# A hybrid decoder block on one core: the last two products of the first up-projection columns trade places, and the weight parts of the first three projections begin at one place

## The chip, the cores and the metric

The kernel runs on one core of a Trainium2 chip. The metric is device time in microseconds (us): the median of several runs of the whole kernel.

## What is computed

One layer of a decoder trunk over 256 tokens and 16 meta tokens (272 rows), width 2048, all in float32. Cut to what matters here:

```python
u = rms_norm(h, g_pre_mix)                      # 272 x 2048
proj = u @ w_in                                 # 2048 x 7168
z_pool, v_conv, g_conv, gate_a, gate_b = split(proj)   # 1024, 1024, 1024, 2048, 2048 columns
y_a = causal_multiscale_pool(z_pool) @ w_pool_out
y_b = conformer_conv(v_conv, g_conv) @ w_conv_out      # 31 taps, layer norm, swish
m = sigmoid(gate_a) * y_a + sigmoid(gate_b) * y_b
h = h + rms_norm(m @ w_o)
f = square(relu(rms_norm(h) @ w_up)) @ w_down   # 2048 x 8192, 8192 x 2048
h = h + rms_norm(f)
```

## The kernel before, in words

**Split numbers.** A float32 matrix is used as two parts. `hi` is the value rounded to a shorter format by a copy on ScalarE (line 178); `lo` is the rest, by a subtraction on VectorE (line 181). A product of two split matrices is the sum of three matmuls: hi times hi, hi times the rest of the activation, lo times hi.

**The stream of weights.** All weights come in the order of one list, `stream` (lines 111 to 134), in chunks of 1 MB (128 partitions by 2048 numbers). `open_chunk` (line 159) takes the next chunk, loads it on SyncE's queue into one of three `raw` buffers, and notes the two split steps; `fetch` (line 198) opens chunks two ahead of the one that it hands out and issues their split steps. The parts live in six rooms, three for `hi` and three for `lo`, used in turn (keys `hi0`, `hi1`, `hi2`, `lo0`, ...). So a chunk's `hi` can be written as soon as TensorE has finished with the chunk three before it.

**Places.** A room is 48 numbers longer than a part, so that the part can begin at one of four offsets. `LINE` is 16 numbers, 64 bytes. `part_tile` (line 152) shifts the part inside the room so that its start, counted in lines of 64 bytes and modulo four (256 bytes), has a chosen value, the same in every room; call it the part's place. Line 155 reads the pair (place of `hi`, place of `lo`) from the table `PLACES`; a chunk that is not in the table gets (1, 1). Line 141 gives every chunk of `w_up` the pair (2, 1). Line 142 gives the first 24 chunks pairs of their own: two chunks make one product of 256 columns, and the product with number p gets (p mod 4, p // 4). The rows of the activation `u` are padded so that all of them begin at one place too.

**The first three projections** are those products: 256 columns each of `v` (convolution values), `g` (convolution gate) and `z` (pool). Their order and their places are

| product | v0 | g0 | v1 | g1 | v2 | g2 | v3 | g3 | z0 | z1 | z2 | z3 |
|---|---|---|---|---|---|---|---|---|---|---|---|---|
| (hi, lo) | 0,0 | 1,0 | 2,0 | 3,0 | 0,1 | 1,1 | 2,1 | 3,1 | 0,2 | 1,2 | 2,2 | 3,2 |

Here the weights stand in the array and the 272 rows of `u` stream past. Each product is 16 blocks of depth by 2 column tiles by 3 matmuls (`mm3`, line 334: `hi` with u's first part, `hi` with its second, `lo` with its first), so 96 matmuls with 272 moving columns. v0 runs interleaved with the transposes that make `u` (lines 442 to 452); the others run in `project` (line 362). Beside them, VectorE works through a list of pending pieces, `drain` handing out one piece after another at points of the program that are fixed when it is built: 240 taps of the convolution (line 405) and the sums of the pooling windows, among others.

**What follows** is a run of wide products (gates, pool and convolution outputs, `w_o`), where the activation stands and 512 weight columns stream (`block_t`, line 590), all with parts at (1, 1); then the MLP, in four passes of `w_up` and `w_down`.

**The up projection** has the weights standing again. The two parts of an activation lie side by side, so that one wide matmul (`mm2_high`, line 342: 512 moving columns) gives both products with `hi`, and a narrow one (`mm2_low`, line 348: 256 columns) adds the product with `lo` to the first half of the accumulator. `mm2` (line 353) issues the wide one and then the narrow one. The first 512 columns of the first pass, `up00`, are written out by hand (lines 892 to 945), because their activation becomes ready piece by piece; their last quarter of the depth is the loop of lines 940 to 945. There each of four accumulators gets four pairs, wide and narrow, and is then evacuated: `halves` (line 378) copies the first half on ScalarE and adds the second on VectorE.

Of the kernel before, what the change touches and what calls it, by code (L numbers as in the profile page):

```python
# [14 lines left out]
P = 128  # L15
# [7 lines left out]
def hybrid_block(ctx: ExitStack, tc: tile.TileContext, ins: dict, out: bass.AP):  # L23
# [7 lines left out]
    KD = D // P  # L31
# [28 lines left out]
    def acc_tile(name):  # L60
        return psA.tile([P, CW], F32, tag="acc", name=name)
# [15 lines left out]
    def flush(n=0):  # L77
        while len(late) > n:
            late.pop(0)()
# [20 lines left out]
    def columns(w, k0, nk, c0, shape=(CK, CW)):  # L100

        ck, cw = shape
        return [(w[(k0 + kc) * P:(k0 + kc + ck) * P, c0:c0 + cw]
                 .rearrange("(k p) c -> p k c", p=P), shape) for kc in range(0, nk, ck)]
# [6 lines left out]
    stream = []  # L111
# [2 lines left out]
            stream += columns(w_in, 0, KD, c0 + h * HALF_CW, HALF)  # L114
    for h in range(PW // HALF_CW):
        stream += columns(w_in, 0, KD, h * HALF_CW, HALF)
    first_products = len(stream)
    standing_chunks = set()
    for n in range(2 * D // CW):
        stream += columns(w_in, 0, KD, G0 + n * CW)  # L120
# [14 lines left out]
    FIRST = KD // HALF[0]  # L135
# [3 lines left out]

    LINE = 16  # L140
    PLACES = {n: (2, 1) for n in standing_chunks}
    PLACES.update({n: (n // FIRST % 4, n // FIRST // 4) for n in range(first_products)})
    KEYS = [f"{tag}{b}" for tag in ("lo", "hi") for b in range(3)]
    ready = {}

# [52 lines left out]
    def fetch(ahead=2):  # L198

        for c in range(ahead + 1):  # L200
            if c == len(opened) and at["n"] < len(stream):
                open_chunk()
            if c < len(opened):
                split_pieces(c)
        flush()
        return opened.pop(0)[:2]
# [135 lines left out]
    def mm2_high(acc, hi, act, k, cs, start, ts=slice(0, T), stop=False):  # L342
        off = act.shape[3] - T
        nc.tensor.matmul(acc.rearrange("p (a t) -> p a t", a=2)[:, :, ts], hi[:, k[0], cs],  # L344
                         act[:, k[1], :, off + ts.start:off + ts.stop], start=start, stop=stop,
                         skip_group_check=True)

    def mm2_low(acc, lo, act, k, cs, stop=False):
        off = act.shape[3] - T
        nc.tensor.matmul(acc[:, :T], lo[:, k[0], cs], act[:, k[1], 0, off:],  # L350
                         start=False, stop=stop, skip_group_check=True)

    def mm2(acc, hi, lo, act, k, cs, first, last):


        mm2_high(acc, hi, act, k, cs, first, stop=last)
        mm2_low(acc, lo, act, k, cs, stop=last)
# [291 lines left out]
    hi, lo = fetch()  # L649
    for g in range(NG):  # L650
        for j in range(GK):
            q = g * GK + j
            acc = acc_tile(f"acc_grp_{q}")[:, :T]
# [158 lines left out]
    u2 = m  # L812
# [28 lines left out]
    def evac_up(j0):  # L841
        def f(j, acc):
            s = halves(acc, f"up_{j0 + j}")
            nc.vector.scalar_tensor_tensor(s, s, 0.0, s, op0=ALU.max, op1=ALU.mult)
            split(f_act[(j0 + j) // (KD // 2)], (j0 + j) % (KD // 2), s)
        return f
# [89 lines left out]
    hi, lo = fetch()  # L936
# [3 lines left out]
    for j, acc in enumerate(accs):  # L940
        for k in range(CK):
            kk = 3 * CK + k
            mm2(acc, hi, lo, u2, (k, kk), slice(j * P, (j + 1) * P), False, kk == KD - 1)
        flush(1)
        evac_up(0)(j, acc)
    ssq2 = const.tile([P, NT, NB], F32, name="ssq2")
# [64 lines left out]
    n = KD // CK - 3  # L1011
    for kc in range(n):
        hi, lo = fetch()
# [54 lines left out]
```

## Time and profile before

| | |
|---|---|
| median of 3 runs | 1237.76 us (1237.73 to 1237.81) |
| the profiled execution: its own time | 1238.2 us |
| its span, first to last instruction | 1236.3 us |
| TensorE matmuls (PE): busy | 1224.7 us (99%), 6572 instructions |
| VectorE (DVE): busy | 807.6 us (65%) |
| ScalarE (ACT): busy | 541.9 us (44%) |
| mean granted clock of TensorE | 0.998 |

The profile lists instructions with start and duration. A matmul's duration is longer than its step: the next one starts before it ends. What a row of matmuls costs is therefore read from start to start, or from the chain of work that ended last, which follows each instruction back to what released it and gives every stretch its length. A busy share says little here: the question is how fast TensorE steps, and whether anything makes it wait.

### The profile page before, as it was taken

How to read it: one execution, taken by the hardware profiler on the slowest of the kernel's cores; microseconds unless marked ns; L12 is line 12 of the kernel's file. 1: busy time of each engine (PE TensorE's matmuls, PEld its weight loads, DVE VectorE, ACT ScalarE, POOL GpSimd, SP SyncE). 2: the span in 40 equal slices, each digit the busy share in tenths (PEclk: the TensorE clock that was granted, in tenths of full speed). 3: DMA queues.
4: the chain of work that ended last, by engine and by line, in shares of the span. 5: the costliest groups of instructions: out<-in, count | busy, mean ns of one | idle time of the engine just before them, and what ended most of it. 6: DMA issues, size and time to landing. Idle time of an engine off the chain costs nothing.

```text
span 1236.3 us, 15686 instructions
## 1 busy us (share of the span) xinstructions
PE 1224.7 (99%) x6572; PEld 1061.3 (86%) x6572; DVE 807.6 (65%) x938; ACT 541.9 (44%) x571; POOL 6.2 (0%) x18
## 2 busy tenths in 40 slices
PE   9999999999999999999999999999999999999997
PEld 7999988888888888898888888888888888888886
DVE  5799988999676654585654556654475544556555
ACT  6533334444584433555433345433344433435432
POOL 1000000000000000000000000000000000000000
PEclk9999999999999999999999999999999999999999
DMA  8655556556548656646556566556566556566551
GB/s 260 207 181 179 171 171 204 188 188 204 175 165 298 212 205 204 204 142 200 175 200 197 183 199 200 180 199 200 185 194 204 182 193 204 176 201 203 187 187 68
DMA packets 130757, 237.22 MB, mean 192 GB/s; under 512 B 3985, under 2 KB 29905, under 8 KB 130160
## 3 DMA queue, kind: packets, MB, share of 16 engines
q1 hardware_dynamic: 128768, 229.78, 57.4%
q0 software_dynamic: 768, 4.35, 0.9%
q10 hardware_dynamic: 1152, 2.11, 0.5%
q8 instruction: 51, 0.84, 0.3%
q14 instruction: 18, 0.15, 0.0%
HBM read 234.12 MB, written 2.10 MB: 191 GB/s over the span
## 4 chain that ended last, share of the span: by engine, by line
PE 98%; DVE 1%; DMA 0%; ACT 0%; DVEq 0%; issue 0%; ACTq 0%
PE acc_dn L595 26%; PE acc_up L344 19%; PE acc_gate L595 14%; PE acc_up L350 10%; PE acc_o L595 5%; PE acc_v L339 4%; PE acc_z L339 4%; PE acc_g L339 4%; PE acc_co L595 4%; PE acc_po L595 4%; PE acc_f_last L595 2%; PE acc_o_last L595 2%; DMA x_in<-in_x_dram 0%; PE xt L286 0%; PE ht L820 0%; PE mt L715 0%
## 5 line engine op out<-in xcount | busy, mean ns | idle before, releaser
L181 DVE TENSOR_TENSOR lo<-raw,hi 128x2048 fp32r<-128x2048 f32 (+1 forms) x236 | 495.1, 2101 | 354.5 <-ACT hi L178 354.1
L178 ACT CAST hi<-raw 128x2048 fp32r<-128x2048 f32 (+1 forms) x236 | 413.7, 1757 | 559.3 <-PE acc_dn L595 190.6
L344 PE MATMUL acc_up<-m,hi 128*128 128x512 f32 (+1 forms) x1008 | 339.1, 387 | 0.0
L595 PE MATMUL acc_dn<-hi,f_act 128*128 128x512 f32 x960 | 296.3, 389 | 0.0
L350 PE MATMUL acc_up<-m,lo 128*128 128x256 f32 x992 | 272.5, 277 | 0.0
L344 PEld LDWEIGHTS acc_up<-m,hi 128*128 128x128 f32 x1008 | 187.0, 188 | 39.5
L595 PEld LDWEIGHTS acc_dn<-hi,f_act 128*128 128x128 f32 x960 | 180.2, 188 | 37.5
L595 PE MATMUL acc_dn<-lo,f_act 128*128 128x512 f32 x480 | 186.8, 389 | 0.0
L350 PEld LDWEIGHTS acc_up<-m,lo 128*128 128x128 f32 x992 | 185.2, 188 | 0.1
L595 PE MATMUL acc_gate<-hi,u 128*128 128x512 f32 x512 | 158.6, 390 | 0.0
L405 DVE SCALAR_TENSOR_TENSOR c<-a,taps,c 128x256 f32<-128x256 f32 x240 | 115.4, 483 | 6.6
L595 PEld LDWEIGHTS acc_gate<-hi,u 128*128 128x128 f32 x512 | 96.1, 188 | 20.0
L595 PEld LDWEIGHTS acc_dn<-lo,f_act 128*128 128x128 f32 x480 | 90.1, 188 | 18.5
L595 PE MATMUL acc_gate<-lo,u 128*128 128x512 f32 x256 | 99.6, 389 | 0.0
L595 PE MATMUL acc_o<-hi,m 128*128 128x512 f32 x192 | 59.6, 390 | 0.0
L595 PEld LDWEIGHTS acc_gate<-lo,u 128*128 128x128 f32 x256 | 48.1, 188 | 10.0
L339 PE MATMUL acc_v<-u,hi 128*128 128x272 f32 x256 | 50.6, 295 | 0.0
L339 PE MATMUL acc_z<-u,hi 128*128 128x272 f32 x256 | 48.6, 289 | 0.0
L339 PE MATMUL acc_g<-u,hi 128*128 128x272 f32 x256 | 48.1, 288 | 0.0
L595 PEld LDWEIGHTS acc_o<-hi,m 128*128 128x128 f32 x192 | 36.0, 188 | 7.4
L595 PE MATMUL acc_co<-hi,s_act 128*128 128x512 f32 x128 | 40.4, 391 | 0.0
L339 PEld LDWEIGHTS acc_z<-u,hi 128*128 128x128 f32 x256 | 40.4, 188 | 0.0
(222 smaller groups left out, 1060.8 us busy)
## 6 DMA issues: line engine op xcount, KB each, us to landing
raw<-in_w_up_dram SPq DMA_DIRECT2D x64, 1024.0 KB, 5.4
raw<-in_w_down_dram SPq DMA_DIRECT2D x64, 1024.0 KB, 5.1
raw<-in_w_in_dram SPq DMA_DIRECT2D x54, 1024.0 KB, 5.1
raw<-in_w_o_dram SPq DMA_DIRECT2D x16, 1024.0 KB, 5.1
raw<-in_w_pool_out_dram SPq DMA_DIRECT2D x8, 1024.0 KB, 5.1
raw<-in_w_conv_out_dram SPq DMA_DIRECT2D x8, 1024.0 KB, 5.2
raw<-in_w_in_dram SPq DMA_DIRECT2D x8, 256.0 KB, 7.7
h<-in_x_dram POOLq DMA_DIRECT2D x1, 2048.0 KB, 11.0
```

The source lines that it names most:

```text
L178: nc.scalar.copy(hi[:, sl, :], raw[:, sl, :])
L181: nc.vector.tensor_sub(lo[:, sl, :], raw[:, sl, :], f32(hi[:, sl, :]))
L339: nc.tensor.matmul(acc, w[:, k[0], cs], act[:, k[1], a, off:], start=first and n == 0, stop=last and n == 2)
L344: nc.tensor.matmul(acc.rearrange("p (a t) -> p a t", a=2)[:, :, ts], hi[:, k[0], cs], act[:, k[1], :, off + ts.start:off + ts.stop], start ...
L350: nc.tensor.matmul(acc[:, :T], lo[:, k[0], cs], act[:, k[1], 0, off:], start=False, stop=stop, skip_group_check=True)
L405: nc.vector.scalar_tensor_tensor(c, conv["a"][:, q, i:i + T], taps[:, q, i:i + 1], c, op0=ALU.mult, op1=ALU.add)
L595: nc.tensor.matmul(acc, act(kk)[:, a_, ts_], w_[:, k, :], start=kk == 0 and n == 0, stop=kk == nk - 1 and n == 2)
```

## The change

The table's second line goes, so that the first 24 chunks get (1, 1) like the rest of the stream. And in the last quarter of `up00`, the last of the four pairs of each accumulator is issued narrow first, then wide; the wide matmul now closes the accumulation.

```diff
     for h in range(PW // HALF_CW):
         stream += columns(w_in, 0, KD, h * HALF_CW, HALF)
-    first_products = len(stream)
     standing_chunks = set()
...
     PLACES = {n: (2, 1) for n in standing_chunks}
-    PLACES.update({n: (n // FIRST % 4, n // FIRST // 4) for n in range(first_products)})
     KEYS = [f"{tag}{b}" for tag in ("lo", "hi") for b in range(3)]
...
     for j, acc in enumerate(accs):
         for k in range(CK):
             kk = 3 * CK + k
-            mm2(acc, hi, lo, u2, (k, kk), slice(j * P, (j + 1) * P), False, kk == KD - 1)
+            cs = slice(j * P, (j + 1) * P)
+            if kk < KD - 1:
+                mm2(acc, hi, lo, u2, (k, kk), cs, False, False)
+            else:
+                mm2_low(acc, lo, u2, (k, kk), cs)
+                mm2_high(acc, hi, u2, (k, kk), cs, False, stop=True)
         flush(1)
         evac_up(0)(j, acc)
```

No instruction is added or taken away. On TensorE four pairs change their order; on the other engines and the queues the order of instructions is what it was. In the changed order the narrow matmul of the first such pair waits for ScalarE's part of the activation and the wide one for VectorE's, where before the wide one waited for both.

## The prediction

> **What bounds the kernel now.** I read the page's chain of work that ended last first, then the same chain in order of time over the first 165 us, where the first three projections run, then what the engines waited for.
>
> ```profile
> PE 98%; DVE 1%; DMA 0%; ACT 0%; DVEq 0%; issue 0%; ACTq 0%
> ```
>
> TensorE's own sequence makes up 98% of the span. A change pays if TensorE steps faster or waits less, and almost nothing else counts. The list of what TensorE waited for shows how little waiting there is to remove:
>
> ```profile
> PE idle L272 <- POOL ident masks.py:199: 1.4, 1, 1.4
> PE xt L286 <- DMA x_in<-in_x_dram: 1.1, 1, 1.1
> PE acc_grp L339 <- DVE y L658: 0.4, 1, 0.4
> ```
>
> Two waits come before the first product and one at 343 us; none is touched by the change. So the question is the step from one matmul to the next. The chain in order of time (start, length, what, count):
>
> ```profile
> 25.51 3.20 PE acc_v L339 x24
> 28.71 12.04 PE acc_g L339 x96
> 40.75 6.05 PE acc_v L339 x48
> 46.80 0.96 PE pb L329 x6
> 47.76 3.03 PE acc_v L339 x24
> 50.80 0.19 PE pv_pool_scale L243
> 50.98 0.61 PE taps_t L464 x8
> 51.59 3.22 PE acc_v L339 x24
> 54.81 12.05 PE acc_g L339 x96
> 66.86 12.14 PE acc_v L339 x96
> 79.01 11.85 PE acc_g L339 x96
> 90.85 12.09 PE acc_v L339 x96
> 102.94 12.05 PE acc_g L339 x96
> 114.99 48.58 PE acc_z L339 x384
> ```
>
> Each x96 row is one product: 96 matmuls of one shape, with 272 moving columns. They are not equally long. g2 takes 11.85 us, 123.4 ns a step; the others 12.04 to 12.15 (z: 48.58 / 4), 125.4 to 126.5 ns. g2 is the product with places (1, 1). So the kernel before holds a table of twelve pairs of places with their times, and the changed kernel uses for all twelve the pair with the shortest row.
>
> **The change, part one: the places.** What is removed is the difference of each product to g2; nothing is added. From the rows, less 11.85: g0 0.19, g1 0.20, v2 0.29, v3 0.24, g3 0.20, g2 nothing, and the four z products 48.58 - 47.40 = 1.18. v1 is cut in three by other work; at 123.4 ns its 48 matmuls would take 5.92 in place of 6.05 (0.13), its 24 take 2.96 in place of 3.03 (0.07); the last 24 follow transposes and carry a restart that stays, so I give them the 0.07 of the equal piece before: 0.27 in all. Together 2.57 us.
>
> v0 is interleaved with transposes. Its plain step stands at its end, after the last transpose; the first and the last row of this stretch of the timeline (start, duration, engine, line), with the first of g0:
>
> ```profile
> 25.91 0.41 PE L339 MATMUL acc_v<-u,hi 128*128 128x272 f32 x2
> ...
> 28.42 0.29 PE L339 MATMUL acc_v<-u,lo 128*128 128x272 f32 x1
> 28.54 0.41 PE L339 MATMUL acc_g<-u,hi 128*128 128x272 f32 x2
> ```
>
> From 25.91 to 28.54 lie 21 matmuls, 125.2 ns each. At 123.4 the 96 of v0 would save 0.17 us if all were plain. Some follow a transpose and are not; the bounds are 0 and 0.17, and I take 0.13, since most steps are plain. Part one: 2.70 us.
>
> Does the gain reach the end? What could hold TensorE up in its place is VectorE, which works beside it on the convolution. From 54.65 to 163.41 us (length, busy), and what it waited for there:
>
> ```profile
> 54.65:163.41 108.76, 101.69 (x156) 1.00 0.53 171
> ```
>
> ```profile
> DVE lo L181 <- ACT hi L178: 3.5, 6, 0.7
> DVE v L412 <- PE acc_v L339: 1.1, 1, 1.1
> DVE g L419 <- PE acc_g L339: 0.3, 1, 0.3
> ```
>
> In this stretch TensorE would gain 0.20 + 0.29 + 0.24 + 0.20 + 1.18 = 2.11 us, and VectorE has 4.9 us of waits for others to give up. It stays just ahead. Nor is a short lateness felt, because the parts are early. The `lo` of one chunk, and the start of z2, which reads it:
>
> ```profile
> 127.06 1.91 ACT L178 CAST hi<-raw 128x2048 fp32r<-128x2048 f32 x1 [4.14 <-PE acc_z L339]
> ```
>
> ```profile
> 129.06 2.28 DVE L181 TENSOR_TENSOR lo<-raw,hi 128x2048 fp32r<-128x2048 f32 x1
> ```
>
> ```profile
> 139.09 0.41 PE L339 MATMUL acc_z<-u,hi 128*128 128x272 f32 x2
> ```
>
> It is done at 131.34 and first read from 139.09 on: 7.7 us of cover. ScalarE stood idle for 4.14 us until TensorE gave the room free, so the load had landed; the loads are no bound either. If VectorE's cover were gone, each later `lo` would cost TensorE its lateness, which is the third rival below. Behind z the chain is TensorE's again: what comes later starts 2.7 us earlier and is as long as before.
>
> Here the Trainium skill speaks against the change. "TensorE: Matmul & The Clock Gate", section "Step-by-step: what each phase is for", says that TensorE reads moving data and weights through two independent ports, so that loading the next weights takes no bandwidth from the running matmul. By that rule the place of the weights should be without effect and the sum would be that of part two alone, near 1237.7 us. The trace disagrees as far as it goes, with 123.4 against 125.4 to 126.5 ns for equal matmuls; no run here shows the ports themselves.
>
> **Part two: the swap.** Four times, "wide, narrow" becomes "narrow, wide". The order before this pair is ...narrow, and behind it comes the next accumulator's wide one. So a step wide to narrow goes, a step narrow to narrow comes, and a step wide to wide comes in place of one narrow to wide.
>
> ```profile
> 533.10 1.92 PE acc_up L350 x16
> ...
> 544.02 0.23 PE acc_up L344
> 544.25 0.12 PE acc_up L350
> 544.38 0.23 PE acc_up L344
> 544.61 0.12 PE acc_up L350
> ```
>
> ```profile
> 617.51 87.06 PE acc_dn L595 x384
> ```
>
> In the mixed order a wide step is 0.23 and a narrow one 0.12 us (x16 narrow: 1.92, the same 0.12). A row of wide ones, with other operands, has 87.06 / 384 = 0.227. So the pair costs the same by the first rows, and some 0.006 us less by the last; four times is 0 to -0.03. In a wide to wide step at this stage the next weights could be read less well, but the trace has no such step; bounded by the nearest difference, that of the places (some 3 ns), it is +0.01. I take -0.02, which does not move the first decimal.
>
> The new waits cost nothing: the pieces of u2 in question are written by VectorE here, before the loop begins at 543.86.
>
> ```profile
> 541.66 1.66 DVE L830 SCALAR_TENSOR_TENSOR m<-ht,vecs,m 128x256 fp32r<-128x256 f32 x4
> ...
> 543.86 0.39 PE L344 MATMUL acc_up<-m,hi 128*128 128x512 f32 x1
> 544.09 0.28 PE L350 MATMUL acc_up<-m,lo 128*128 128x256 f32 x1
> ```
>
> They end at 543.32. The evacuation now waits for a wide matmul that starts 0.12 after its narrow one and lasts 0.39 (0.51), where it waited for a narrow one that starts 0.23 after and lasts 0.28 (0.51): no difference.
>
> **The sum.** -2.70 - 0.02 = -2.7 us. The profiled execution took 1238.2 us by its own time (span 1236.3), 0.4 above the median of the runs; with the change it would be 1235.5 (span 1233.6). Against the median, 1237.76 - 2.7 = 1235.1 us.
>
> **The rivals.**
>
> 1. *The place is not the cause.* Only one product stands at (1, 1), and it might owe its time to when it runs. Then only part two counts: 1237.7. Against it: g0, g1 and g3 run with less and more beside them and agree within 0.01 us, so what lies beside hardly matters, while g2 between them differs by 0.2. Chance 5%. (The skill's rule of two ports, above, comes out here.)
>
> 2. *One pair, but not in every room.* g2 used two of the three rooms; how the third does at (1, 1) with this shape is not shown. If it steps like the average of the rest, 8 of 24 chunks gain nothing: 1237.76 - 1.8 = 1236.0. Against it: the wide products use all three rooms at (1, 1) in rotation, and 384 of them average 0.227 without a hitch. 6%.
>
> 3. *VectorE becomes the bound.* If some of its waits are hand-over times that it can't give up, it falls behind by up to 2.1 us, and if the cover did not absorb that, half of the gain would go: 1236.4. Against it: 7.7 us of cover, and VectorE waits again for 7.7 us in all between 163 and 203 us, where it would catch up:
>
> ```profile
> DVE lo L181 <- ACT hi L178: 7.7, 6, 3.1
> ```
>
> 8%.
>
> 4. *Slower: writes meet reads.* While g2 ran, the `hi` being written stood at place 2. In the changed kernel ScalarE and VectorE write parts at the very places from which TensorE reads. If such a meeting cost as much as the worst place costs over the best (126.5 - 123.4 = 3.1 ns) on top of the worst, a step would be 129.6 ns: (129.6 - 126.0) x 1152 matmuls = 4.1 us more, 1241.9. It turns slower than before once the mean step passes 126 ns. Against it: the wide products write and read at (1, 1) already. In the gate stage, with VectorE busy for nearly all of the time, and in the down projection, with far less beside it, they step alike: 146.91 / 648 and 87.06 / 384 are both 0.2267.
>
> ```profile
> 163.57 146.91 PE acc_gate L595 x648
> ```
>
> 3%.
>
> **How the numbers follow.** The forecast, 1234.8 to 1235.6 by the bounds of v0, of v1's last piece and of the swap, has the remaining 78%. To 1236.6 the range takes in rivals 2 and 3; it leaves out rivals 1 and 4 and tails on both sides, less than 2 in 10. A measurement of this kernel can tell about 0.2% (2.5 us) from no change, and the forecast, 0.22%, lies close to that edge: of its 78% I put 72 beyond 1235.28 and 6 within. Rivals 1, 2 and 3 (19%) are within too, but for 1% of them that I move to a loss I do not see; rival 4 is slower: faster 0.72, same 0.24, slower 0.04.
>
> **What would show it.** In the chain of the changed kernel every x96 row of g and v should read 11.85 and z 47.4 for its x384; the gates should begin near 160.9 in place of 163.57, v0 giving its share ahead of 28.71. If the rows are short but the gates begin no earlier, TensorE waits, and the list of its waits names VectorE or ScalarE (rival 3). If one chunk in three stays long, it is rival 2; if all stay at 12.05 to 12.15, rival 1; if all grow, rival 4. Behind the gates every stretch should keep its length, and the loop of `up00` should be within 0.05 us of what it was. I would be wrong if the place's effect hung on something that this table does not vary.

## The result, and the profile after

The changed kernel takes 1234.69 us in the median, 1237.82 before in the same runs; the ratio is 0.9972, with an interval of 0.9962 to 0.9982. So it is faster, by 3.1 us or 0.25% by the medians, where 2.7 were forecast. Both 1234.69 and the time by the ratio, 0.9972 x 1237.76 = 1234.3 us, lie a little under 1234.8, the low end of the forecast. The ratio is lower than that of the medians (0.9975); one of the ten executions of before took 1243.03 us, while the other nine took 1237.55 to 1238.16. The profiled execution has a span of 1233.1 us, 3.2 under that of before. (In the changed file a line of before behind 142 has a number lower by two, up to the loop: L337 is `mm3`, L342 the wide and L348 the narrow matmul of `up`, L593 `block_t`.)

The chain of work of the changed kernel, in order of time, over the first three projections:

```profile
25.71 3.17 PE acc_v L337 x24
28.88 11.84 PE acc_g L337 x96
40.72 5.92 PE acc_v L337 x48
46.64 0.96 PE pb L327 x6
47.60 2.97 PE acc_v L337 x24
...
54.53 11.84 PE acc_g L337 x96
66.38 11.84 PE acc_v L337 x96
...
101.89 11.84 PE acc_g L337 x96
113.73 47.36 PE acc_z L337 x384
161.09 4.09 PE acc_gate L593 x18
```

Every product of 96 matmuls reads 11.84. From the first g row to the gates it is 161.09 - 28.88 = 132.21 us, where before it was 163.57 - 28.71 = 134.86: 2.65 less. TensorE waits for the same three as before; only the wait for the load of `x` is now in two parts, and the second of them, 0.15 us, lies within v0:

```profile
PE idle L270 <- POOL ident masks.py:199: 1.4, 1, 1.4
PE xt L284 <- DMA x_in<-in_x_dram: 0.5, 2, 0.4
PE acc_grp L337 <- DVE y L656: 0.4, 1, 0.4
```

and VectorE, in the stretch that ends where the gates begin, still has 2.4 of its 4.9 us of waits:

```profile
DVE lo L179 <- ACT hi L176: 1.7, 6, 0.4
DVE v L410 <- PE acc_v L337: 0.7, 1, 0.7
```

The other part of the gain lies where none was expected. From the gates to the end it took 1236.3 - 163.57 = 1072.7 us before and takes 1233.1 - 161.09 = 1072.0 now: 0.7 less. It is all in one place, between the first matmul of the hand-written loop and the down projection of the first pass. Of the changed kernel, the first matmul in the timeline and the row of the down projection in the chain:

```profile
541.34 0.39 PE L342 MATMUL acc_up<-m,hi 128*128 128x512 f32 x1
```

```profile
614.30 87.10 PE acc_dn L593 x384
```

That is 72.96 us, against 617.51 - 543.86 = 73.65 before, for the 32 matmuls of the loop and the 384 of the three products behind it (`up01` to `up03`), which the change does not touch. Read from start to start in the timeline, each of the three takes 22.40 us in place of 22.61: a pair of wide and narrow takes 350 ns in place of 353.3. Here is the second of them (`up02`) from its first matmul to the next product's, before and then after: window, length, busy time and instructions of PE, PEld, DVE, ACT and POOL, granted clock, DMA share, GB/s.

```profile
572.13:594.74 22.61, 22.61 (x131) 19.66 (x129) 13.53 (x17) 12.61 (x21) 0.00 (x0) 1.00 0.61 186
```

```profile
569.34:591.74 22.40, 22.40 (x131) 19.71 (x130) 13.54 (x17) 12.60 (x21) 0.00 (x0) 1.00 0.61 187
```

The clock is 1.00 in both, and VectorE, ScalarE and the DMAs do the same beside it. So neither the clock nor the work of the others is what differs.

The profile of before already had the sign that a pair's step is no constant. The chain of before, one pass later:

```profile
704.58 0.23 PE acc_up L344
...
791.64 87.06 PE acc_dn L595 x384
```

Four products, 256 pairs, in 791.64 - 704.58 = 87.06 us: 340 ns a pair. Matmuls of the same shapes with parts at the same places step at 353.3 ns in the first pass and at 340 in the second, third and fourth.

### The profile page after: what moved, and what is told of

The parts are those of the page before. It is cut to its first block, busy times and chain, and to the rows that moved or that the text cites. A ratio compares the mean times of both kernels' runs of the same rounds, so it can differ in the third digit from the quotient of the medians.

```text
span 1233.1 us, 15685 instructions
## 1 busy us (share of the span) xinstructions
PE 1222.1 (99%) x6572; PEld 1059.6 (86%) x6572; DVE 807.6 (65%) x938; ACT 541.6 (44%) x571; POOL 6.1 (0%) x18
## 4 chain that ended last, share of the span: by engine, by line
PE 98%; DMA 1%; DVE 1%; ACT 0%; ACTq 0%; DVEq 0%; issue 0%
PE acc_dn L593 26%; PE acc_up L342 19%; PE acc_gate L593 14%; PE acc_up L348 10%; PE acc_o L593 5%; PE acc_v L337 4%; PE acc_g L337 4%; PE acc_z L337 4%; PE acc_co L593 4%; PE acc_po L593 4%; PE acc_f_last L593 2%; PE acc_o_last L593 2%; DMA x_in<-in_x_dram 1%; PE ht L818 0%; PE mt L713 0%; PE xt L284 0%
## 5 line engine op out<-in xcount | busy, mean ns | idle before, releaser
L342 PE MATMUL acc_up<-m,hi 128*128 128x512 f32 (+1 forms) x1008 | 338.0, 387 | 0.0
L593 PE MATMUL acc_dn<-hi,f_act 128*128 128x512 f32 x960 | 296.4, 389 | 0.0
L348 PE MATMUL acc_up<-m,lo 128*128 128x256 f32 x992 | 272.2, 278 | 0.0
L342 PEld LDWEIGHTS acc_up<-m,hi 128*128 128x128 f32 x1008 | 186.8, 188 | 38.3
L593 PEld LDWEIGHTS acc_dn<-hi,f_act 128*128 128x128 f32 x960 | 180.2, 188 | 37.5
L593 PE MATMUL acc_dn<-lo,f_act 128*128 128x512 f32 x480 | 186.9, 389 | 0.0
L348 PEld LDWEIGHTS acc_up<-m,lo 128*128 128x128 f32 x992 | 185.7, 188 | 0.5
L593 PE MATMUL acc_gate<-hi,u 128*128 128x512 f32 x512 | 158.6, 390 | 0.0
L593 PEld LDWEIGHTS acc_gate<-hi,u 128*128 128x128 f32 x512 | 96.1, 188 | 20.0
L593 PEld LDWEIGHTS acc_dn<-lo,f_act 128*128 128x128 f32 x480 | 90.1, 188 | 18.5
L593 PE MATMUL acc_gate<-lo,u 128*128 128x512 f32 x256 | 99.6, 389 | 0.0
L593 PE MATMUL acc_o<-hi,m 128*128 128x512 f32 x192 | 59.6, 390 | 0.0
L593 PEld LDWEIGHTS acc_gate<-lo,u 128*128 128x128 f32 x256 | 48.1, 188 | 9.8
L337 PE MATMUL acc_v<-u,hi 128*128 128x272 f32 x256 | 49.8, 293 | 0.0
L337 PE MATMUL acc_g<-u,hi 128*128 128x272 f32 x256 | 47.5, 287 | 0.0
L337 PE MATMUL acc_z<-u,hi 128*128 128x272 f32 x256 | 47.4, 287 | 0.0
L593 PEld LDWEIGHTS acc_o<-hi,m 128*128 128x128 f32 x192 | 36.0, 188 | 7.4
L593 PE MATMUL acc_co<-hi,s_act 128*128 128x512 f32 x128 | 40.4, 392 | 0.0
L337 PEld LDWEIGHTS acc_v<-u,hi 128*128 128x128 f32 x256 | 39.8, 188 | 0.4
```

The lines of the kernel that those rows point to most:

```text
L337: nc.tensor.matmul(acc, w[:, k[0], cs], act[:, k[1], a, off:], start=first and n == 0, stop=last and n == 2)
L593: nc.tensor.matmul(acc, act(kk)[:, a_, ts_], w_[:, k, :], start=kk == 0 and n == 0, stop=kk == nk - 1 and n == 2)
```

## The experiments

The runs below were made on three chips, four kernels on the first, four on the second and two on the third, each time with executions of the kernel before beside them. A product's or a pair's step is always read from start to start in the trace of one execution.

The places and the swap were first taken apart; two more kernels make only some of the four swaps.

**The places alone.**

```diff
-            if kk < KD - 1:
-                mm2(acc, hi, lo, u2, (k, kk), cs, False, False)
-            else:
-                mm2_low(acc, lo, u2, (k, kk), cs)
-                mm2_high(acc, hi, u2, (k, kk), cs, False, stop=True)
+            mm2(acc, hi, lo, u2, (k, kk), cs, False, kk == KD - 1)
```

> The changed kernel with the swap taken back, so only the places are changed. Theory (two separate gains): the twelve products read 11.84 us each as in the changed kernel, the gates begin some 2.5 us earlier than before, and the three up products behind the hand-written columns are back at 22.61 us each, so the whole is about 2.6 us under before and some 0.6 us over the changed kernel. Rival (the shorter up products come from what ran earlier, not from the swap): they stay at 22.40 us, and the whole is as fast as the changed kernel.

Measured: 1234.69 us, ratio 0.9977 (0.9967 to 0.9986). The twelve products read 11.84. But the three up products took 22.40 us each without any swap, from the loop's first pair on:

```profile
540.86 0.39 PE L342 MATMUL acc_up<-m,hi 128*128 128x512 f32 x1
```

```profile
613.83 87.10 PE acc_dn L593 x384
```

72.97 us, as in the changed kernel. So the theory that the swap by itself gives the 0.6 us has fallen. The ten times lie in two groups, 1234.3 to 1234.5 and 1234.8 to 1235.9, some 0.6 apart, as if some executions had stepped at 350 and some at 353.3; only one of them was traced.

**The swap alone**, on the kernel before.

> The kernel before with the swap alone. Theory: the twelve products keep their 12.04 to 12.15 us, but the three up products behind the hand-written columns fall from 22.61 to 22.40 us each, so the whole is some 0.7 us under before, where the prediction gave the swap 0.02 us. Rival (the swap is worth nothing by itself): these products stay at 22.61 us and the whole is as before.

Measured: 1236.29 us, ratio 0.9991 (0.9981 to 1.0). The median says little, for the times lie in two groups: five from 1234.8 to 1235.7 and five from 1236.9 to 1237.6. The traced execution (1237.18) entered the loop at 353.3 and left it at 350; its products are at 22.40. Five of the others took some 2 us less, which neither the theory nor the rival had foreseen.

**The swap on the first two accumulators, and on the first one only** (there `j >= 1`).

```diff
-            if kk < KD - 1:
-                mm2(acc, hi, lo, u2, (k, kk), cs, False, False)
+            if kk < KD - 1 or j >= 2:
+                mm2(acc, hi, lo, u2, (k, kk), cs, False, kk == KD - 1)
```

> The changed kernel, but only the first two of the four accumulators end narrow, wide; the other two end wide, narrow as before. Theory (a rhythm of steps, once set, carries on while wide and narrow alternate without a break): in the changed kernel the third accumulator starts with pairs of 226 + 114 = 340 ns, the rhythm of the later passes, and its own swap ends that. Without the last two swaps the 340 ns should last through the three following products, 21.76 us each in place of 22.40: some 1.9 us under the changed kernel, about 5 us under before. Rival (each swap saves by itself): half of the swap's gain is lost, the three products lie between 22.40 and 22.61 us, and the whole is some 0.3 us over the changed kernel.

> The changed kernel with the swap on the first accumulator alone. Theory (rhythm): after the first swap the changed kernel steps at 231 + 117 and 233 + 119 ns, 350 ns a pair, so with no further swap the three following products should be near 22.40 us each, as in the changed kernel, and the whole within 0.2 us of it. Rival (each swap saves by itself): a quarter of the gain, the three products near 22.56 us, the whole 0.5 us over the changed kernel.

Measured: two swaps 1232.57 us (ratio 0.9969, 0.9956 to 0.9982), the times 1232.5 three times, 1234.83, 1235.74; one swap 1232.96 us (0.9968, 0.9956 to 0.9981), the times 1232.4 to 1233.1 four times, 1234.3 and 1234.5. Both forecasts of where the traces would end were wrong, and the traces say why. The timeline of the kernel with one swap, its first two accumulators:

```profile
540.77 0.39 PE L342 MATMUL acc_up<-m,hi 128*128 128x512 f32 x1
541.00 0.28 PE L348 MATMUL acc_up<-m,lo 128*128 128x256 f32 x1
541.12 0.40 PE L342 MATMUL acc_up<-m,hi 128*128 128x512 f32 x1
541.35 0.28 PE L348 MATMUL acc_up<-m,lo 128*128 128x256 f32 x1
541.47 0.39 PE L342 MATMUL acc_up<-m,hi 128*128 128x512 f32 x1
541.70 0.40 PE L348 MATMUL acc_up<-m,lo 128*128 128x256 f32 x2
541.94 0.63 PE L342 MATMUL acc_up<-m,hi 128*128 128x512 f32 x2
...
542.53 0.39 PE L342 MATMUL acc_up<-m,hi 128*128 128x512 f32 x1
542.75 0.28 PE L348 MATMUL acc_up<-m,lo 128*128 128x256 f32 x1
542.87 0.39 PE L342 MATMUL acc_up<-m,hi 128*128 128x512 f32 x1
543.09 0.28 PE L348 MATMUL acc_up<-m,lo 128*128 128x256 f32 x1
543.21 0.39 PE L342 MATMUL acc_up<-m,hi 128*128 128x512 f32 x1
```

The pairs before the swap (the rows with x2) start 0.35 apart, behind it 0.34: 540.77, 541.12, 541.47; then 542.53, 542.87, 543.21. It stays at 340 ns through the three products; loop and products take 611.71 - 540.77 = 70.94 us, 2.7 less than before:

```profile
611.71 87.06 PE acc_dn L593 x384
```

Call a step that lasts while the pairs alternate a rhythm. There are three of them here, 353.3, 350 and 340 ns a pair, and a swap moves the stream on from one to the next, 353.3 to 350 to 340 to 353.3. Read so, all the traces agree in which single swaps are the only breaks, later ones as well:

| kernel, traced execution | swaps | rhythm on entry, and behind each swap | up01 to up03, each |
|---|---|---|---|
| before | 0 | 353.3 | 22.61 us |
| changed | 4 | 353.3, 350, 340, 353.3, 350 | 22.40 |
| places alone | 0 | 350 | 22.40 |
| swap alone | 4 | 353.3, 350, 340, 353.3, 350 | 22.40 |
| two swaps | 2 | 350, 340, 353.3 | 22.61 |
| one swap | 1 | 350, 340 | 21.76 |
| places (3, 2), below | 4 | 353.3, 350, 340, 353.3, 350 | 22.40 |
| places (., 3), below | 4 | 350, 340, 353.3, 350, 340 | 21.76 |

Nineteen swaps in six traces, and each moved the rhythm the same way: seven from 353.3 to 350, seven from 350 to 340, five from 340 to 353.3. Between two swaps a rhythm shows in only three pairs; behind the last it lasts for 192 or more. The circle was read off the traces of the changed kernel and of the next three with a swap, eleven swaps; it stood on record before the eight of the last two. It also sorts most of the groups of times. An execution enters at 353.3 or at 350; with one swap it leaves at 350 or 340, which differ by 192 pairs x 10 ns = 1.9 us, and its groups are 1.9 apart; with two it leaves at 340 or 353.3, 2.6 us apart, and the groups are 2.3 and 3.2 apart; with four, on the kernel before, at 350 or 340, and the groups lie some 2 apart.

Two things do not fit without more. Two executions of before, in the later rounds, took 1235.19 and 1235.47 us where the others took 1236.9 to 1238.3; an entry at 340 would explain them, but neither was traced. And none of the ten executions of the changed kernel took near 1232.4 us, as an entry at 350 should make it (350 to 340 over four swaps), though with two swaps and with one, by the groups, six of eleven entered at 350. Up to the first swap the three kernels issue the same instructions. So how often each entry occurs is not the same in every round of runs, and what sets it is not known.

**All at one other place.**

```diff
     PLACES = {n: (2, 1) for n in standing_chunks}
+    PLACES.update({n: (3, 2) for n in range(24)})
```

> The changed kernel with its 24 first chunks all at the pair (3, 2), the pair of z3 before, in place of (1, 1). Theory (the pair itself decides): each of the eleven uninterrupted products takes z3's 12.16 us, so the projections lose some 0.3 us each against the changed kernel, 3.7 us in all, and the whole is about 1 us slower than before apart from what the up products do. Rival (what helps is that all chunks begin at one place, whichever it is): the products take 11.84 us as in the changed kernel.

Measured: 1235.86 us, ratio 0.9985 (0.9975 to 0.9995). Neither held (L338 is `mm3` here):

```profile
54.22 11.95 PE acc_g L338 x96
...
78.11 11.95 PE acc_g L338 x96
...
113.95 47.78 PE acc_z L338 x384
```

The products take 11.95 us, where z3 with this pair took 12.16 by its starts in the timeline. Being all at one place is not what makes 11.84; but a pair has no fixed length either. What ran before a product seems to matter here too.

**A run of wide matmuls**, to set the rhythm in every execution alike.

```diff
     for j, acc in enumerate(accs):
         for k in range(CK):
...
+            mm2_low(acc, lo, u2, (k, 3 * CK + k), slice(j * P, (j + 1) * P))
+    for j, acc in enumerate(accs):
+        for k in range(CK):
+            mm2_high(acc, hi, u2, (k, 3 * CK + k), slice(j * P, (j + 1) * P), False,
+                     stop=k == CK - 1)
         flush(1)
         evac_up(0)(j, acc)
```

> The places of the changed kernel; in the hand-written loop all sixteen narrow matmuls come first, then the sixteen wide ones in a row, accumulator by accumulator, each evacuated after its last. Theory (three rhythms of 353.3, 350 and 340 ns a pair; the one that a run is in is settled by small waits ahead of the loop, one swap moves it on by one, 353.3 to 350 to 340 to 353.3, and it lasts while pairs alternate): passes two to four always come out of a run of wide matmuls, the down projection, and always step at 340. A run of sixteen wide ones should set 340 here too, in every execution: the three up products 21.76 us each, the whole near 1232.4 us with little spread, 5.2 us under before. Rival (the 340 ns belong to the later passes for another reason, and a run of wide ones does not set it): the three products at 22.40 or 22.61 us, and the whole at 1234.4 to 1235.1, or in two or three clusters as in the runs with one and two swaps.

Measured: 1234.77 us, ratio 0.9975 (0.9965 to 0.9984), all nine times between 1234.46 and 1235.09. One group, as expected, but it is the wrong rhythm: the trace shows 350 ns, 22.40 us a product. The run does not set 340. In it the wide steps were 231 and 236 ns in turn, where those of the down projection are 227. That the places make this difference is not shown: the down projection has its parts at (1, 1), but its weights also stream past where those of the up projection stand. Nor does the one group prove that the run wipes out the entry, for on this chip 21 of 24 executions of before lie in one group too, 1237.4 to 1238.1.

**The same on the last accumulator alone**: three accumulators as before, the last with four narrow and then four wide ones.

> The places of the changed kernel; the first three accumulators end as before, the last one takes its four narrow matmuls first and then its four wide ones. Theory as for the run of sixteen, but this asks how long the run must be. If four wide ones in a row settle the rhythm, the three up products take 21.76 us in every execution, the whole near 1232.5 us. If the step of narrow to narrow and of wide to wide only moves the rhythm on, by three places here (which is back to where it was), they take 22.40 or 22.61 us, and the whole 1234.4 to 1235.1.

Measured: 1234.57 us, ratio 0.9974 (0.9964 to 0.9984), nine times from 1234.25 to 1235.15. The trace entered at 353.3 and left at 350. Four wide ones did not settle 340; whether they wipe out the entry is not told by these times, whose spread would hold both rhythms that follow.

**The chunks of `w_up` at (1, 1) as well.**

```diff
-    PLACES = {n: (2, 1) for n in standing_chunks}
+    PLACES = {}
```

This stands on the kernel with the places alone.

> The changed kernel without the swap, and the chunks of the up projection too at (1, 1) in place of (2, 1). Theory (the rhythms belong to a pair of places): passes two to four step at something else than 340 ns a pair, longer if (2, 1) was a good pair, and the first pass no longer shows 353.3 or 350. Rival (the rhythms have nothing to do with places): 340 in passes two to four, 350 or 353.3 in the first, the whole as with the places alone, 1234.4 to 1235.1.

Measured: 1243.99 us, ratio 1.0049 (1.0031 to 1.0068), 9.3 us over the places alone. The rhythms depend on the places: a pair now steps at 346.7 ns in the first pass (22.19 us a product) and at 353 in the second (22.61), where (2, 1) gave 353.3 or 350 and then 340. The very pair that is best for the 272-column products is bad for the alternation of wide and narrow in the later passes, which outweighs what it gains in the first.

**Run, then one swap**: the first two accumulators get eight narrow and then eight wide matmuls, the third ends narrow, wide, the fourth as before.

```diff
+    for j in range(2):
+        for k in range(CK):
+            mm2_low(accs[j], lo, u2, (k, 3 * CK + k), slice(j * P, (j + 1) * P))
     for j, acc in enumerate(accs):
         for k in range(CK):
...
-            if kk < KD - 1:
-                mm2(acc, hi, lo, u2, (k, kk), cs, False, False)
+            if j < 2:
+                mm2_high(acc, hi, u2, (k, kk), cs, False, stop=kk == KD - 1)
+            elif kk < KD - 1 or j == 3:
+                mm2(acc, hi, lo, u2, (k, kk), cs, False, kk == KD - 1)
             else:
```

> The places of the changed kernel; in the hand-written loop the first two accumulators get their eight narrow matmuls first and then their eight wide ones, the third ends narrow, wide, the fourth as before. Theory (the run of wide ones at these places did not set 340, but it set 350 in the trace and left a single cluster of times, so it wipes out where the execution came from; one swap behind it then moves 350 on to 340): the three up products take 21.76 us each in every execution, the whole 1232.3 to 1232.9 us with no second cluster, about 5 us under before and 2 us under the changed kernel. Rival (the single cluster was chance; the run passes on whatever rhythm came in): two or three clusters, at 1232.4, 1234.4 and 1235.1.

Measured: 1232.4 us, ratio 0.996 (0.9947 to 0.9974), five times from 1232.21 to 1233.09. As expected: one group, and the trace steps at 340 ns behind the swap.

```profile
540.82 1.11 PE L348 MATMUL acc_up<-m,lo 128*128 128x256 f32 x8
541.77 2.26 PE L342 MATMUL acc_up<-m,hi 128*128 128x512 f32 x9
...
544.57 0.40 PE L348 MATMUL acc_up<-m,lo 128*128 128x256 f32 x2
544.80 0.63 PE L342 MATMUL acc_up<-m,hi 128*128 128x512 f32 x2
...
545.39 0.39 PE L342 MATMUL acc_up<-m,hi 128*128 128x512 f32 x1
545.62 0.28 PE L348 MATMUL acc_up<-m,lo 128*128 128x256 f32 x1
545.73 0.39 PE L342 MATMUL acc_up<-m,hi 128*128 128x512 f32 x1
545.96 0.28 PE L348 MATMUL acc_up<-m,lo 128*128 128x256 f32 x1
546.07 0.39 PE L342 MATMUL acc_up<-m,hi 128*128 128x512 f32 x1
```

545.39, 545.73, 546.07: 340 ns a pair. By the medians this is the quickest of the kernels, 5.35 us under before and 2.3 us under the changed one; the lower group of the kernel with one swap, from 1232.4 on, is as quick. That it is one group rests on five times, beside which 14 of 15 executions of before lay in one group as well (1237.5 to 1238.3), and the next kernel's, on the same chip, in two.

**The four pairs that before did not hold**: (0, 3) to (3, 3), three times over.

```diff
+    PLACES.update({n: (n // 2 % 4, 3) for n in range(24)})
```

> The changed kernel with the twelve first products at (0, 3), (1, 3), (2, 3), (3, 3), three times over: the four pairs that the kernel before did not hold. It asks whether a pair is better than (1, 1), and whether a pair has one length. Theory (a pair has a few rhythms, and which one a product falls into depends on the product before it too, as (3, 2) showed with 12.16 and 11.95): products with the same pair after the same neighbour agree, all lie between 11.84 and 12.2 us, none below. Rival (a pair has one length, and (3, 2) was read wrongly): each pair one value in all three turns, and some pair may be under 11.84.

Measured: 1236.55 us, ratio 0.9992 (0.9982 to 1.0002). No pair beats (1, 1): by their starts, (0, 3) takes 12.08 us, (1, 3) 12.02, (2, 3) 12.16, (3, 3) 12.16. Equal pairs behind equal neighbours agree within 0.002 us. The one that came behind the interleaved v0 differs, 12.05 for the first (1, 3) against 12.02 for the other two. So both readings hold in part: one length a pair in a settled sequence, moved a little by how it was entered. Its times are in two groups, 1235.3 to 1235.7 and 1237.4 to 1237.7, as four swaps make them.

## Why the prediction was right and wrong

**Right: the places, by their mechanism and nearly in size.** "What is removed is the difference of each product to g2" gave 2.57 us without v0; the chain shows 2.65. The kernel with the places alone shows the same rows without the swap. Every row fell to g2's length, in all three rooms, so rivals 1 and 2 are out. VectorE kept waits to spare, so rival 3 is out, and parts written at the places that are read cost nothing that the rows show, so rival 4 is out too. The kernel with the places alone stands at 0.9977 (0.9967 to 0.9986). One part of it was luck: the prediction took the one row of a pair for the length of twelve. For (1, 1) that held. For (3, 2) it would have failed, with 12.16 us in the row of before and 11.95 when all products stood there. Why (1, 1) is the quickest is open.

**Wrong in sign, small: v0.** I took 0.13 us off. Interleaved with transposes, ten blocks of v0 take 13.33 us in the chain (12.38 to 25.71), where ten took 13.27 before (12.24 to 25.51), and only the plain end is shorter, 3.17 in place of 3.20. The whole of v0 is no shorter: from its first matmul to g0's it takes 19.40 us with the wait of 0.15, 19.21 in the kernel with the places alone, and 19.20 before. My lower bound was 0.

**Wrong: "-0.02" for part two, and "what comes later starts 2.7 us earlier and is as long as before".** I priced each kind of neighbours (narrow to narrow, wide to wide) by a step of its own, as if a step were the property of two matmuls, and let the price end with the loop. The loop's own part was indeed small, 0.06 us. But the stream of pairs keeps a rhythm once it is in one, and a break in the alternation moves it to the next. In the traced execution four swaps took 353.3 to 350, and 192 untouched pairs behind the loop carried it: 192 x 3.3 ns = 0.64 us. That is the missing term. The spans add up with it: 2.65 from g0 to the gates and 0.7 behind them, less the 0.17 us by which g0 starts later, are the 3.2 us. The warning stood in the profile of before: equal shapes at equal places with 340 ns a pair in three passes and 353.3 in one. I read the two kinds of rows and did not ask why they differ.

**What the 0.6 us are not.** They are not a fixed gain of the swap. The kernel with the places alone has the same median, 1234.69 us; its traced execution entered at 350 by itself, and by its groups of times some others did too. Which rhythm an execution enters with is settled ahead of the loop. In the four traces that entered at 350, one step between two transposes (line 820 of before) some 5 us earlier, where TensorE is held up by a little, is 142 ns; in the five that entered at 353.3 it is 144 ns or more. That is an agreement and not a proof, and no run tried to set this wait. In the traces of the two kernels whose loop opens with a run of narrow and wide matmuls it is 144 and 159 ns; by this sign neither entered at 350, and neither shows what such a run does with that entry. What in TensorE keeps the rhythm is open as well.

**The two ports.** By the Trainium skill's rule of two independent ports ("TensorE: Matmul & The Clock Gate", "Step-by-step: what each phase is for"), as the prediction took it, the place of the weights should have had no effect, and the time would have been that of rival 1. The section speaks of bandwidth, not of where an operand begins. The rows speak against it as a rule for the step: equal products took 11.84 to 12.16 us by their places, and (1, 1) for the up projection cost 9.3 us. No run shows the ports themselves.

## What to carry to other kernels

Where TensorE never waits, look at the step from start to start and compare equal stretches of the program: if the same shapes step differently in two passes, or at two offsets of the operands within 256 bytes, there may be time to gain without removing an instruction. A break in a regular alternation of matmuls may cost nothing where it stands and change the step of everything behind it, so measure the whole stretch up to the next change of shape. And where single times fall into groups, trace executions of both before trusting a median: here a kernel's gain of 0.6 us was a matter of which group an execution fell into. Opening the loop with a fixed run and one swap gave one group, and the quick one, in the five executions taken.

## What the runs showed of the hardware that was not expected

- For one pair of places, the pairs of a wide (512) and a narrow (256) matmul have at least three lasting rhythms, 353.3, 350 and 340 ns, kept over 192 pairs without a slip. One exchange of the order moved them on in a fixed circle, 19 times out of 19 (places (2, 1) alone).
- Places matter to each shape differently: (1, 1) is the best of the pairs seen for 272 columns (11.84 us, the others 11.95 to 12.16), and for the alternation of 512 and 256 it is worse than (2, 1) in the later passes (353 against 340 ns) and better in the first (346.7 against 350 or 353.3).
- Writing parts at the same places from which TensorE reads has no price that these traces show: all products step at 11.84 us whatever ScalarE and VectorE write beside them.
